# Four moved steps and a staging slot in a two-layer streaming encoder (RG-LRU layer, then forgetting attention)

## The chip, the cores and the metric

One core of a Trainium2 chip runs one program. The metric is the device time of one execution in microseconds (us). Engines are named as in the profile: PE (TensorE matmul), PEld (its weight loads), DVE (VectorE), ACT (ScalarE), POOL (GpSimd), SP (SyncE, which issues every DMA of this kernel). Each engine works through one queue, in order.

## What is computed

Two layers over a prompt of 2048 tokens and a sample group of 32 tokens, D = 1024. Each layer has modulation vectors made from a conditioning vector, a norm ahead and a norm behind:

```python
for i in range(2):
    sh, sc, gt = split3(silu(c) @ ada_w[i] + ada_b[i])       # modulation: 6 blocks n of 512 columns
    h = rmsnorm(x, norm_pre[i]) * (1 + sc) + sh
    if i == 0:  # RG-LRU: h @ w_in, conv4, gates, scan, silu gate, @ lru_w_out
        y = rglru(h)
    else:       # forgetting attention, 16 heads of 64
        q, k, v, g, fl = split(h @ fox_w_in)
        s = q @ k.T * scale + cum_q - cum_k                   # causal
        y = (softmax(s) @ v * silu(g)) @ fox_w_out            # sample group: 512 cached rows as well
    x = x + gt * rmsnorm(y, norm_post[i])
```

The sequence, the final state of the recurrence, k, v and log f are outputs.

## The kernel before

Every float32 operand of a large product is split into a high and a low part (`hi_*` on POOL, ACT or DVE, `lo_dve` on DVE, line 104), and a product is three matmuls.

The program is written as Python generators that yield after each piece of work, and a driver takes steps from them in turn. That fixes the order in which instructions are written down. The framework then lays out each engine's queue from its own planned times: whatever it expects to be ready may go ahead of what was written earlier, and what was written earlier wins when both are ready. Semaphore waits and buffer slots (named groups of equal buffers: `half` 5, `ahalf` 11, `raw` 3, `w` 5, `h` 32, `od` 5) are laid out by it too. The queues are then fixed, and an engine that reaches an instruction whose input is late stands still.

The stages in order of time:

- 0 to 100 us: constants and four modulation blocks of layer 0 (`ada`).
- about 60 to 740 us: `lru_in`, 12 column groups n for each half of the prompt, in chunks (2 a group in the first half, 3 in the second) of 48 matmuls. Beside the chunks `side` takes steps of other generators: `mod`, the other six modulation blocks (`ada`, two of layer 0, four of layer 1), and `cache_parts`. In the second half `mod` gives two steps a chunk for 16 steps and then one. A block is eight steps, one for each k; `finish` closes it: ACT copies a part out of PSUM (line 262), DVE adds twice (263, 264), and then either PE transposes the block (273) for `shv` and `gsv`, or a DMA and a product follow (n of 4 and 5). All these blocks accumulate in the one bank `pvb`.
- 740 to 1080 us: `out_tiles` of layer 0 (line 765), with the norm of layer 1.
- 1074 to 2673 us: the projections of layer 1, `proj` for each half: four groups of a v unit (line 1020) and six k, q, g units (1059). A v unit writes each of its token tiles to two staging buffers (lines 1028 and 1029, ACT) that two DMAs read (1036, 1037). The first 16 steps run before the second set of buffers is opened. Weights of the second half come in pairs, one buffer `w` and one `raw` a unit (line 952).
- 1160 to 2838 us: `attention`, merged with the projections: 8 pairs of heads p, two heads e, two query units of 512 for each half; a tile is 128 keys (lines 1239 to 1297). At the end of a unit `fin_steps` lists steps with a number of tiles to wait: `s0` copies out, `d0` and `d1` move the row of denominators through DRAM to 128 partitions (lines 1323, 1326), `rc` takes the reciprocal on DVE (1330), `d2` and `d3` send it back (1333, 1336), `zz` and `zy` multiply on POOL (1347, 1351). `sample_steps` is the same chain for the sample group (lines 1452, 1456, 1459, 1462, 1466). Whenever the next pair's projections are not done, attention starts again with loads, `LOAD_STEPS` steps of the projections, and then its maxima (1205, 1208).
- 2600 to 2716 us: `load_wout` brings the eight rows of the last matrix (line 689), splits each on ACT or POOL into `h` buffers (95, 98) and DVE (104). `out_tiles` follows (loads of line 736, split on ACT), its first seven tiles beside the attention, the rest up to the end.

Of the kernel before, what the change touches and what calls it, by code (L numbers as in the profile page):

```python
# [10 lines left out]
F32R = mybir.dt.float32r  # L11
# [24 lines left out]

V_STEPS = 16

LOAD_STEPS = 18

N_H, N_W, N_RAW, N_HALF, N_AH = 32, 5, 3, 5, 11
N_C, N_WG = 12, 2
# [12 lines left out]
def hybrid_kernel(ctx, tc, io):  # L55
# [15 lines left out]
    def get(role, shape, dt=F32):  # L71

        pool_, tag, bufs = roles[role]
        return pool_.tile(shape, dt, name=nm(tag), tag=tag, bufs=bufs)

    def set_roles(pool_, tag, bufs, *names):
        for n in names:
            roles[n] = (pool_, tag, bufs)

    def hs(shape, dt=F32):  # L80
        return get("half", shape, dt)
# [151 lines left out]
    def ada(layer, ns, acc, bank, ahead=3, whole=lambda i: False):  # L233
# [26 lines left out]
        def finish(n, ps, mod):  # L260
            lo = get("ab", [2, 512])
            act.activation(lo, ps[32:34, :], AF.Copy)
            dve.tensor_tensor(mod, mod, ps[0:2, :], ALU.add)
            dve.tensor_tensor(mod, mod, lo, ALU.add)
            if n >= 4:
                c = slice(512 * (n - 4), 512 * (n - 4) + 512)
                sp.dma_start(lo, io["npost"][layer:layer + 1, c].partition_broadcast(2))
                dve.tensor_tensor(mod, mod, lo, ALU.mult)
                sp.dma_start(gp_d[layer, :, c], mod)
                return  # L270
            pt = bank()
            for j in range(4):
                pe.transpose(pt[:, 2 * j:2 * j + 2], mod[:, 128 * j:128 * j + 128], ident[0:2, 0:2])
            ks = slice(4 * (n % 2), 4 * (n % 2) + 4)
            pt = pt[:, 0:8].rearrange("p (k g) -> p k g", g=2)
            if n < 2:
                dve.tensor_copy(shv[layer][:, ks, :], pt)
            else:
                for g in range(2):
                    dve.scalar_tensor_tensor(gsv[layer][:, ks, g], pt[:, :, g], 1.0, npre[:, layer, ks],  # L280
                                             ALU.add, ALU.mult)
# [11 lines left out]
        for i, (n, k) in enumerate(todo):  # L293
            split(i + 1)
            load(i + ahead)
            if k == 0:
                ps = acc()
            ws = parts.pop(i)
            for j, w in enumerate(ws):
                pe.matmul(ps[0:34, :], (scf if len(ws) == 1 else scs)[:, k, :], w,  # L300
                          start=k + j == 0, stop=k == KD - 1 and j == len(ws) - 1)
            if k == 3 and n not in mods:
                bias(n)
            if k == KD - 1:
                finish(n, ps, mods.pop(n))
                del ps
            yield 2 * 216

    def load_gp(layer, sample):
# [199 lines left out]
    def run(gen):  # L509
        while True:  # L510
            try:
                next(gen)
            except StopIteration as e:
                return e.value
# [167 lines left out]
    def load_wout(src, kn, w, ahead=0):  # L682
# [2 lines left out]

        def load(k):
            if k < kn:
                raw[k] = get("raw", [128, D])
                sp.dma_start(raw[k], src[128 * k:128 * k + 128, :])

        for k in range(ahead):
# [27 lines left out]
    def out_tiles(tiles, kn, zsrc, xsrc, dst, gps, bank, w, release=True, pause=0.0, post=None):  # L719
# [25 lines left out]
                zq[i][j] = (a, b)  # L745

        load(0)
        yield 2 * pause
        yield 2 * pause
        split(0)  # L750
        yield 0.0
        end = None
# [171 lines left out]
    def proj(half, h, bank):  # L924
# [66 lines left out]
        fl = None  # L991
        for i, (kind, p) in enumerate(run_units):
            ws = wsp.pop(i)
            if i == len(run_units) - 1:
                flags.add(("last", half))
                yield 0.0

# [5 lines left out]
            if kind == "v":  # L1003
# [7 lines left out]
                for t in range(nt):  # L1011
# [3 lines left out]
                    for k in range(KD):  # L1015
# [7 lines left out]
                            yield 6 * 108  # L1023
                        if c == 12:
                            drain()
                    vt, v2 = hs([128, 4, 64]), hs([128, 4, 2, 64], F32R)
                    pv = ps[:m, :256].rearrange("p (h d) -> p h d", d=64)
                    act.activation(v2[:m, :, 1, :], pv, AF.Copy)
                    act.activation(vt[:m], pv, AF.Copy)
# [78 lines left out]
    def attention(kbs, qms, vss, smp, bst, bmx, bpva, bpvb):  # L1108
# [192 lines left out]
        def fin_steps(u):  # L1301
# [34 lines left out]
                sp.dma_start(pairs[key][1][r0:r0 + 64, :], dd[1:2, :].partition_broadcast(64))  # L1336

            g = GAP[j.half]
            steps = [(0, s0), (1, d0), (1 + g, d1), (1 + 2 * g, rc), (2 + 2 * g, d2), (2 + 3 * g, d3)]
            if e == 1:  # L1340
                def ldg():
                    u.sg = get("od", [128, nq])
# [6 lines left out]
                def zy():  # L1349
# [2 lines left out]
                    sp.dma_start(z2_d[j.p, :, u.q0:u.q0 + nq], O)  # L1352
                    if u is j.last:
                        flags.add(("z", j.half, j.p))
                steps += [(2 + 2 * g, ldg), (2 + 4 * g, zz), (3 + 4 * g, zy)]
            return steps


# [2 lines left out]
        def sample_steps(p, e):  # L1361
# [106 lines left out]
            def zz():  # L1468
# [3 lines left out]
                sp.dma_start(z2_d[p, :, SEQ:TOK], O)  # L1472

            steps = [(0, load_k), (0, load_q), (1, load_v), (4, maxima), (5, fin), (7, fin2), (9, scores), (11, low),
                     (12, products), (13, s0), (14, d0), (17, d1), (20, rc), (21, d2), (24, d3)]
            return steps + ([(27 if p == NP - 1 else 32, ldg), (27 if p == NP - 1 else 36, zz)] if e else [])


# [166 lines left out]
    with tc.tile_pool(name="first", bufs=1) as first:  # L1645
# [2 lines left out]
        set_roles(big, "half", N_HALF, "ab")  # L1648
        set_roles(big, "ahalf", N_AH, "z", "zs", "xn", "hf")
        set_roles(big, "h", N_H, "aw")  # L1650
        set_roles(big, "ahalf", N_AH, "cx")
        setup()
        lc = setup_lru(first)
# [54 lines left out]
        rest[:] = run(blocks)  # L1708
        run(load_h(h, ha_d, 1, 512, 512 + NS))
        blocks, parts = later, cache_parts()  # L1710
        run(side(until(blocks, ("free", 0, 1, 0)), [[(islice(mod, 16), 2), (mod, 1)], [(parts, 2)]]))
        for _ in range(4):
            next(wout)
        rest = run(blocks)
# [7 lines left out]
        last = ada(1, (4, 5), bpvb, bank0, ADA_LAST, lambda i: True)  # L1722
        for _ in range(4):
            next(wout)
        next(out)
        next(out)
        for fn in rest:
# [38 lines left out]
    set_roles(second, "od", N_OD, "od")  # L1766
    set_roles(big, "raw", N_RAW, "z")
    set_roles(big, "w", N_W, "zs", "gp")
    set_roles(big, "half", N_HALF, "hf")
    att = {}  # L1770
    last_banks = cycle(bst, bst, bpj, bpj)

# [3 lines left out]
    def main():  # L1776
# [12 lines left out]
            yield next(b)  # L1789
        yield from until(b, ("last", 1))  # L1790
        w = [{}, {}]
        wout = load_wout(io["w3"], NP, w, 2)
        yield next(wout)
        yield from b
        yield from wout
# [104 lines left out]
```

## Time and profile before

| | |
|---|---|
| median of 3 runs | 3016.19 us (3014.15 to 3018.24) |
| profiled execution | 3012.26 us, span 3010.5 us |
| PE busy | 2860.8 us, 95% of the span |
| DVE, ACT, POOL busy | 61%, 49%, 42% |
| DMA | 548 MB, 182 GB/s in the mean |

A row of the windows view gives a stretch's length, each engine's busy time (with the number of its instructions), the granted TensorE clock as a share of 2.4 GHz, the DMA engines' busy share and the rate. A row of the timeline gives start, duration, engine (SPq is SP's queue, a DMA issue), line, operation, out<-in, shape and count; in brackets the engine's idle time before it and what ended it.

### The profile page before, as it was taken

Reading aid. Unit: us, or ns where it says so; the run is one execution under the profiler, and the core shown is the slowest. Engines: PE = TensorE matmul, PEld = TensorE weight load, DVE = VectorE, ACT = ScalarE, POOL = GpSimd, SP = SyncE. Lnnn points to the kernel's source line nnn. Section 1 sums busy time; section 2 is a strip of 40 time slices with the busy share of each in tenths; the row PEclk is TensorE's granted clock in tenths of the full one; section 3 lists DMA queues with packets and bytes.
Section 4 is the critical chain, followed back from the end, with each engine's and each line's share of the span. In section 5 each row is a group of like instructions: output and inputs, shape, how many; then the busy total and the mean of one; then the engine's idle time right before and its main releaser. Section 6 shows DMA issues by size and latency. Waiting matters only on the chain. (4 is left out here: it accounts for less than half of the span.)

```text
span 3010.5 us, 45166 instructions
## 1 busy us (share of the span) xinstructions
PE 2860.8 (95%) x14948; PEld 2290.1 (76%) x14948; DVE 1843.2 (61%) x3282; ACT 1488.2 (49%) x2996; POOL 1257.2 (42%) x1156
## 2 busy tenths in 40 slices
PE   6999999999999989999999999999999999989998
PEld 3777888888676777777777778887888888856686
DVE  7678767777633335646464575676666766677422
ACT  6565544455444423534353443565665656556411
POOL 5444434333322222434343332554555545556522
PEclk8999999999999999999999999999999999999999
DMA  7655586444644598676767865676556655555343
GB/s 262 225 202 203 180 280 212 155 152 138 194 150 139 173 316 253 196 236 193 233 189 228 252 195 176 142 193 162 140 159 152 172 157 154 130 138 123 89 147 97
DMA packets 407002, 548.40 MB, mean 182 GB/s; under 512 B 77096, under 2 KB 241064, under 8 KB 406768
## 3 DMA queue, kind: packets, MB, share of 16 engines
q1 hardware_dynamic: 406768, 545.50, 60.4%
q8 instruction: 119, 1.95, 0.3%
q14 instruction: 115, 0.94, 0.1%
HBM read 333.13 MB, written 212.22 MB: 181 GB/s over the span
## 5 line engine op out<-in xcount | busy, mean ns | idle before, releaser
L1268 POOL TENSOR_TENSOR ahalf<-ahalf,ahalf 128x512 f32<-128x512 f32 (+2 forms) x528 | 586.4, 1111 | 411.6 <-ACT ahalf L1245 400.4
L1059 PE MATMUL pj<-h,w 128*128 128x512 f32 (+1 forms) x2304 | 593.6, 364 | 0.0
L1245 ACT ACTIVATE ahalf<-st 128x512 fp32r<-128x512 f32 (+3 forms) x640 | 341.7, 534 | 386.8 <-PE st L1243 324.1
L104 DVE TENSOR_TENSOR ahalf<-st,ahalf 128x512 fp32r<-128x512 f32 (+3 forms) x640 | 386.6, 605 | 206.1 <-ACT st L1246 179.5
L1059 PEld LDWEIGHTS pj<-h,w 128*128 128x128 f32 x2304 | 423.6, 190 | 85.4 <-issue 0.6
L1208 DVE TENSOR_REDUCE mxs<-mx 128x1 f32<-128x512 f32 (+3 forms) x640 | 371.4, 604 | 132.4 <-PE mx L1205 87.0
L1246 ACT ACTIVATE st<-st 128x512 f32<-128x512 f32 (+3 forms) x640 | 339.5, 530 | 0.0
L1239 PE MATMUL st<-ahalf,kv 128*128 128x512 f32 (+3 forms) x640 | 246.3, 385 | 32.0 <-DVE ahalf L104 30.7
L1291 PE MATMUL pva<-ahalf,vs 128*128 128x512 f32 (+3 forms) x640 | 241.8, 389 | 11.0 <-ACT ahalf L1245 7.3
L1243 PE MATMUL st<-ahalf,kb 96*128 96x512 f32 (+3 forms) x640 | 243.4, 386 | 4.1 <-ACT ahalf L1226 3.7
L1020 PE MATMUL pj<-w,h 128*128 128x256 f32 (+3 forms) x1296 | 229.6, 289 | 11.2 <-DVE flog L1035 6.5
L1205 PE MATMUL mx<-kb,qm 96*128 96x512 f32 (+3 forms) x640 | 224.8, 382 | 7.8 <-DMA qm<-q_d 3.3
L1292 PE MATMUL pvb<-ahalf,vs 128*65 128x512 f32 (+3 forms) x640 | 228.4, 366 | 3.2 <-DVE od L1320 2.1
L573 PE MATMUL pj<-h,w 128*128 128x512 f32 (+1 forms) x1032 | 224.5, 366 | 0.6 <-DVE h L104 0.3
L1020 PEld LDWEIGHTS pj<-w,h 128*128 128x128 f32 (+1 forms) x1296 | 191.5, 189 | 22.5 <-issue 8.6
L573 PEld LDWEIGHTS pj<-h,w 128*128 128x128 f32 x1032 | 174.7, 189 | 32.6 <-DVE h L104 1.3
L573 PE MATMUL st<-h,wg 128*128 128x512 f32 (+1 forms) x840 | 187.6, 377 | 2.3 <-DVE wg L104 1.5
L1059 PE MATMUL pj<-h,raw 128*128 128x272 f32 (+1 forms) x576 | 188.5, 327 | 0.0
L104 DVE TENSOR_TENSOR w<-raw,w 128x1024 fp32r<-128x1024 f32 (+2 forms) x61 | 86.6, 1420 | 153.5 <-ACT w L95 92.0
L104 DVE TENSOR_TENSOR ahalf<-ahalf,ahalf 128x512 fp32r<-128x512 f32 (+2 forms) x183 | 143.4, 785 | 57.9 <-POOL ahalf L98 25.5
L1239 PEld LDWEIGHTS st<-ahalf,kv 128*128 128x128 f32 x640 | 121.6, 190 | 74.4 <-DVE ahalf L104 53.8
L573 PEld LDWEIGHTS st<-h,wg 128*128 128x128 f32 x840 | 147.8, 192 | 32.1 <-DVE wg L104 2.7
(330 smaller groups left out, 5566.2 us busy)
## 6 DMA issues: line engine op xcount, KB each, us to landing
wp_d<-w SPq DMA_DIRECT2D x60, 512.0 KB
vs<-v_d SPq DMA_DIRECT2D x96, 256.0 KB
kv<-k_d SPq DMA_DIRECT2D x192, 128.0 KB
ahalf<-q_d SPq DMA_DIRECT2D x192, 128.0 KB
raw<-in_w SPq DMA_DIRECT2D x44, 512.0 KB
hb_d<-wg SPq DMA_DIRECT2D x32, 512.0 KB
v_d<-half SPq DMA_DIRECT2D x64, 256.0 KB
raw<-wp_d SPq DMA_DIRECT2D x30, 512.0 KB
```

What stands on the lines that cost most here:

```text
L104: dve.tensor_tensor(o, i, f(h), ALU.subtract)
L573: pe.matmul(ps[:, :b - a], l, cols(r, a, b), start=i == 0, stop=i == 23)
L1020: pe.matmul(ps[:m, :nw], l, r, start=c == 0, stop=c == 23)
L1059: pe.matmul(ps[:, :b - a], l, cols(r, a, b), start=c == 0, stop=c == 23)
L1208: dve.tensor_reduce(u.mxs[:sw, si, c:c + 1], ps[:sw, :kw], axis=AX.X, op=ALU.max)
L1239: pe.matmul(ps[:kw, c0:nq], j.ka[k0 // 512][:, kc:kc + kw], u.qa[:, c0:nq], start=True, stop=False)
L1243: pe.matmul(ps[:kw, c0:nq], j.kb[k0 // HALF][0:96, kd:kd + kw], u.qb[0:96, c0:nq], start=False, stop=True)
L1245: act.activation(ph[:kw, c0:nq], ps[:kw, c0:nq], AF.Exp, scale=0.125)
L1246: act.activation(ps[:kw, c0:nq], ps[:kw, c0:nq], AF.Exp, scale=0.125)
L1268: pool.tensor_tensor(u.acc[:kw, c0:nq], f(ph)[:kw, c0:nq], u.acc[:kw, c0:nq], ALU.add)
L1291: pe.matmul(u.pva[:, c:nq], vs[:kw, 0:128], ph[:kw, c:nq], start=ti == 0, stop=last)
L1292: pe.matmul(u.pvb[0:65, c0:nq], vs[:kw, 64:129], pl[:kw, c0:nq], start=ti == 0, stop=False)
```

## The change

Seven edits. (1) `ada`: `finish` ends after its additions, and a new `finish2` does the rest one step later; a block is nine steps, and `mod` now gives two steps a chunk for 26 steps. (2) The v unit's staging buffers have a role of their own, `vst`: slots `ahalf` in the first 16 steps, `half` as before after them. (3) `rc` and all that follows it stand three tiles later in the list, in the second half and for the sample group (not for its last pair). (4) `LOAD_STEPS` 18 to 24. (5) `load_wout` for the last matrix asks for three rows ahead, even rows in `w` slots, and starts one unit earlier. (6) `out_tiles` has a third pause between its first load and its first split; layer 0 takes the third step at once. (7) The flag "last" is set a unit earlier, which is what starts (5).

```diff
-LOAD_STEPS = 18
+LOAD_STEPS = 24
@@ ada: finish
             dve.tensor_tensor(mod, mod, lo, ALU.add)
+            return lo
+
+        def finish2(n, mod, lo):
             if n >= 4:
...
             if k == KD - 1:
-                finish(n, ps, mods.pop(n))
+                mod = mods.pop(n)
+                lo = finish(n, ps, mod)
                 del ps
+                yield 0.0
+                finish2(n, mod, lo)
+                del mod, lo
             yield 2 * 216
@@ load_wout: load
-                raw[k] = get("raw", [128, D])
+                raw[k] = get("w" if ahead and k % 2 == 0 else "raw", [128, D])
@@ out_tiles
         load(0)
-        yield 2 * pause
-        yield 2 * pause
+        for _ in range(3):
+            yield 2 * pause
         split(0)
@@ proj
-            if i == len(run_units) - 1:
+            if i == len(run_units) - 2:
                 flags.add(("last", half))
...
-                    vt, v2 = hs([128, 4, 64]), hs([128, 4, 2, 64], F32R)
+                    vt, v2 = get("vst", [128, 4, 64]), get("vst", [128, 4, 2, 64], F32R)
@@ attention: fin_steps
-            steps = [(0, s0), (1, d0), (1 + g, d1), (1 + 2 * g, rc), (2 + 2 * g, d2), (2 + 3 * g, d3)]
+            a = 1 + 2 * g + (3 if j.half else 0)
+            steps = [(0, s0), (1, d0), (1 + g, d1), (a, rc), (a + 1, d2), (a + 1 + g, d3)]
...
-                steps += [(2 + 2 * g, ldg), (2 + 4 * g, zz), (3 + 4 * g, zy)]
+                steps += [(a + 1, ldg), (a + 1 + 2 * g, zz), (a + 2 + 2 * g, zy)]
@@ attention: sample_steps
-                     (12, products), (13, s0), (14, d0), (17, d1), (20, rc), (21, d2), (24, d3)]
+                     (12, products), (13, s0), (14, d0), (17, d1)]
+            steps += [(20, rc), (21, d2), (24, d3)] if p == NP - 1 else [(23, rc), (24, d2), (27, d3)]
             return steps + ([(27 if p == NP - 1 else 32, ldg), (27 if p == NP - 1 else 36, zz)] if e else [])
@@ driver
+        set_roles(big, "ahalf", N_AH, "vst")
...
-        run(side(until(blocks, ("free", 0, 1, 0)), [[(islice(mod, 16), 2), (mod, 1)], [(parts, 2)]]))
+        run(side(until(blocks, ("free", 0, 1, 0)), [[(islice(mod, 26), 2), (mod, 1)], [(parts, 2)]]))
...
+        next(out)
...
-    set_roles(big, "half", N_HALF, "hf")
+    set_roles(big, "half", N_HALF, "hf", "vst")
...
-        wout = load_wout(io["w3"], NP, w, 2)
+        wout = load_wout(io["w3"], NP, w, 3)
```

## Rows read from the trace of the kernel before

**Rows 1.** The page's first part: engines, busy time, share of the span.
```profile
PE 2860.8 (95%) x14948; PEld 2290.1 (76%) x14948; DVE 1843.2 (61%) x3282; ACT 1488.2 (49%) x2996; POOL 1257.2 (42%) x1156
```

**Rows 2.** Windows around six stops of PE; columns as in the profile section.
```profile
472.00:490.00 18.00, 14.21 (x92) 13.85 (x91) 10.21 (x16) 3.99 (x9) 5.12 (x4) 0.81 0.54 170
560.00:574.00 14.00, 10.71 (x70) 10.18 (x69) 7.90 (x10) 3.23 (x7) 3.57 (x2) 0.88 0.38 125
1088.00:1110.00 22.00, 15.46 (x106) 15.08 (x105) 3.83 (x12) 3.35 (x9) 7.14 (x21) 0.84 1.01 336
1805.00:1816.00 11.00, 7.73 (x53) 7.27 (x51) 2.85 (x6) 0.80 (x2) 0.00 (x0) 0.84 0.51 156
2638.00:2656.00 18.00, 12.17 (x43) 9.19 (x42) 9.43 (x15) 6.46 (x12) 6.67 (x6) 0.81 0.64 173
2704.00:2722.00 18.00, 12.46 (x44) 8.85 (x44) 10.71 (x21) 7.65 (x14) 9.18 (x10) 0.81 0.60 124
```

**Rows 3.** Timeline, 476 to 567 us: the ends of two modulation blocks.
```profile
479.72 0.58 PE L273 MATMUL pj<-ident,half 2*128 2x2 f32 x4 [3.79 <-DVE half L264]
...
562.81 3.15 DVE L626 TENSOR_TENSOR c<-c,c 128x1024 f32<-128x1024 f32 x1
...
566.79 0.63 PE L300 MATMUL pvb<-ahalf,scs 128*34 128x512 f32 x2 [3.29 <-DVE half L263]
```

**Rows 4.** Windows, second half of the LRU layer: two modulation steps a chunk, then one.
```profile
380.00:460.00 80.00, 76.42 (x421) 64.32 (x420) 55.29 (x66) 36.13 (x49) 30.90 (x26) 1.00 0.80 280
460.00:720.00 260.00, 251.07 (x1518) 226.18 (x1517) 186.31 (x268) 133.81 (x199) 92.17 (x69) 0.98 0.48 159
```

**Rows 5.** Timeline, 1099 to 1103 us: first v unit.
```profile
1099.49 0.39 ACT L1029 ACTIVATE half<-st 128x256 f32<-128x256 f32 x1 [6.18 <-DMA out_v_o<-half]
...
1102.76 1.47 PE L1020 MATMUL pj<-w,h 128*128 128x272 f32 x5 [5.34 <-DVE flog L1035]
```

**Rows 6.** Timeline, 2638 to 2712 us: the last matrix and the first tile's load.
```profile
2638.89 0.46 SPq L689 DMA_DIRECT2D raw<-in_w  x1
...
2644.00 0.62 POOL L98 TENSOR_SCALAR h<-raw 128x512 fp32r<-128x512 f32 x1 [6.06 <-DMA raw<-in_w]
...
2701.72 0.42 SPq L736 DMA_DIRECT2D raw<-z_d  x1
...
2711.58 1.06 ACT L95 ACTIVATE w<-raw 128x1024 fp32r<-128x1024 f32 x1 [5.40 <-DMA raw<-z_d]
```

**Rows 7.** Line 952 by operation: durations in ns, first and last start.
```profile
L952 SPq DMA_DIRECT2D w<-wp_d x32: 319/469/637, 1660.6 to 2522.1; - x32
L952 SPq DMA_DIRECT2D raw<-wp_d x32: 319/416/1397, 1662.5 to 2574.0; - x32
```

**Rows 8.** Timeline, 2434 to 2503 us: reciprocal chains of two units.
```profile
2434.92 0.34 SPq L1466 DMA_DIRECT2D tiny<-sg_d  x1
...
2436.27 0.30 SPq L1459 DMA_DIRECT2D dns_d<-rc  x1
...
2436.67 0.37 SPq L1326 DMA_DIRECT2D rc<-dn_d  x1
...
2442.38 0.18 DVE L1330 RECIPROCAL rc<-rc 128x4 f32<-128x4 f32 x1 [3.72 <-DMA rc<-dn_d]
...
2500.82 0.34 SPq L1326 DMA_DIRECT2D rc<-dn_d  x1
...
2502.76 0.30 SPq L1459 DMA_DIRECT2D dns_d<-rc  x1
```

**Rows 9.** Windows around seven waits of line 1330: one of them, and their sum.
```profile
2438.00:2452.00 14.00, 11.82 (x69) 10.40 (x69) 6.88 (x14) 6.66 (x14) 6.88 (x8) 0.88 0.60 124
...
sum 74.00, PE 63.48 PEld 53.45 DVE 32.78 ACT 35.95 POOL 37.27; mean PE 9.07 PEld 7.64 DVE 4.68 ACT 5.14 POOL 5.32
```

**Rows 10.** Timeline, 1810 us: the first maximum of the second half.
```profile
1810.30 0.76 PE L1205 MATMUL mx<-kb,qm 96*128 96x512 f32 x1 [3.27 <-DMA qm<-q_d]
```

**Rows 11.** Waits of POOL, 1838 to 2840 us: total, times, longest.
```profile
POOL od L1347 <- DMA od<-dn_d: 2.5, 2, 1.3
```

## Prediction

> **What bounds the kernel now.** I read the page first: PE is busy for 95% of the span, the next engine for 61% [rows 1]. The sum of PE's work is not touched by any edit, so only PE's standing time is at stake, and the time it spends at half clock after a stop. Next I listed every idle stretch of PE over 0.6 us with what ended it, and looked at the largest in the windows view. The reader is to take two numbers from a window: its length less PE's busy time, and one less the granted clock, times the length. The second is what the lower of the two clock levels (1.2 instead of 2.4 GHz) cost there, for at half speed half of the time is lost: a clock of 0.81 over 18 us is 6.8 us at half, 3.4 us lost. Each stop is then followed back in the timeline to the instruction that came late.
>
> **1. Modulation blocks in two steps.** At 479.72 PE stood 3.79 us before the transposes of line 273, because DVE's additions came late; at 566.79 it stood 3.29 us before the next block's first matmul, which needs the bank `pvb` that the late addition still reads [rows 3]. DVE was late because a product that it works on beside POOL took 3.15 us [rows 3]. With the clock the two cost 3.79 + 3.42 and 3.29 + 1.68: 12.2 us [rows 2]. In the new order a step, in this stretch a chunk of 5.5 to 10 us of matmuls (48 of 272 or 512 columns), stands between the additions and the transposes, and one more before `pvb` is wanted; both exceed the lateness. PE is always supplied there (251.07 us of 260 [rows 4]), so the planner has no idle moment into which it would pull the transposes forward. I count 85%: 10.4 us. The first four blocks run with nothing between the steps, so nothing changes there. What `finish2` takes along (the DMAs and the product for n of 4 and 5, DVE's copies for the rest) is wanted after 740 us at the earliest; the cover is the rest of the LRU layer.
> The price is the pace: six blocks take 54 steps instead of 48, and 13 chunks instead of 8 take two. The eight chunks at two steps left PE idle for 3.58 us, 0.45 each; the slower stretch after it for 8.93, of which 7.08 are the two stops, leaving 0.07 for each of some 25 chunks [rows 4]. Five chunks more at 0.38: 1.9 us.
>
> **2. Staging slots.** Two buffers a tile out of five `half` slots hold two tiles. At 1099.49 ACT had stood 6.18 us until a DMA out of such a buffer had landed, and PE 5.34 us for the bank behind it [rows 5]; the window's loss is 6.54 + 3.52 = 10.1 us [rows 2]. Four tiles now go to `ahalf`, whose other users there (layer 0's last tiles) are done by then. But DMA is full in this stretch (share 1.01 [rows 2]), so the landings stay late, and tiles 5 to 8 have the five slots again. I take 7; bounds 3 (one of the two stops) and 10.1.
>
> **3. Last matrix, and the pause before the first split.** A row's load issued at 2638.89 was waited for by POOL until 2644.00 [rows 6]; DVE and then PE stood behind that, 5.83 + 3.42 = 9.3 us [rows 2]. The load was late because `raw` has three slots and the last projection weights took them up to then; these loads run out at 2522.1 for `w` and only at 2574.0 for `raw` [rows 7]. Even rows in `w` are thus loaded long before their buffers in `h` come free, and odd rows get a `raw` slot one row sooner. The number of rows ahead alone would matter little, as SP issues what has a slot. 85%: 7.9 us.
> The next stop is the tile load of 2701.72, for which ACT stood 5.40 us until 2711.58 [rows 6]; PE lost 5.54 + 3.42 = 9.0 us [rows 2]. Its `raw` slot comes free earlier now, but the load took 9.9 us and ACT came to it after 4.5: where the load moves, the planner's place for ACT moves too, unless the `w` slots that the split writes to, now shared with four rows, hold it back. One third: 3.0 us. The third pause only moves the split in the written order.
>
> **4. `LOAD_STEPS`.** One restart shows a stop: 3.27 us for `qm` [rows 10], with the clock 5.0 [rows 2]. That maximum had been pulled ahead of written projections, so six more steps may or may not move it. One third: 1.7. Elsewhere the longer pause is filled by projections.
>
> **5. Reciprocals three tiles later.** Seven units in the second half show DVE standing at line 1330 (3.72 us in the one shown [rows 8]) and PE behind it. The seven windows have 74 less 63.48 = 10.5 us of idle PE, and three of them a dip of 1.68 us [rows 9]: 15.6 us. Is it won? The lists give tiles, but the queues do not keep them: the load of line 1466 stands at place 32 of its list and was issued at 2434.92, ahead of line 1459, which stands at 21 [rows 8]. What is ready goes first, and rc becomes ready by the planner's reckoning soon after `d1`, in the old list and in the new. What the seven have in common is another thing: line 1326 was issued 0.4 us after line 1459's write, and its data let DVE go only 5.7 us later; where it went first (2500.82 before 2502.76) DVE did not wait [rows 8]. The edit moves both alike. I take 0, bounds 0 and 15.6.
> The Trainium skill (DMA: Bandwidth & Descriptors, Queues, rings and completion order) says that a DMA's semaphore increment lands only after every earlier write of that DMA engine; the trace agrees, 5.7 us behind the write and no wait where the read went first [rows 8]. By that rule too the stop goes only if the two change places.
>
> **The sum.** 10.4 + 7 + 7.9 + 3.0 + 1.7 = 30.0. Less 1.9 for the pace, and 2 for new small stops, an estimate from the 2 us that PE idled in the slower stretch of [rows 4]: 26. The profiled execution took 3012.26 us (span 3010.5); 2986 against it. The median of the runs lies 3.9 us above that execution: 2990.
>
> **Rivals.**
> (a) Reciprocals do come late enough: all 15.6 us as well, 2974. For it: seven stops of one kind, 3.72 us in the one shown, and three tiles are more: the two issues of line 1326 shown are 28 tiles and 64.2 us apart, 2.3 us a tile, 6.9 for three [rows 8]. Against it: [rows 8]. The skill's page on DMA (Rules for kernel authors) says to issue early and to wait late, which would give this time; the trace does not show that the place in the list is where the wait falls. 13%.
> (b) The waits are dealt again. Every queue after 380 us is planned anew; loads that land later than planned stop an engine elsewhere. Then of 3 to 5 nothing stays, of 1 and 2 10.4 + 7, and half of those 17.4 us is given back in new stops of the kind of [rows 10]: some 8 us won, 3008. For it: DMA times of 5 to 10 us against places planned after 4.5. Against it: slots and a chunk of matmuls are real room, whatever the order. 19%.
> (c) Slower: the products `zz` on POOL. They follow `d3`, which follows rc. Now POOL waits for them twice, 2.5 us in all, in 1000 us [rows 11]. If rc, `d2` and `d3` do move by three tiles (6.9 us) while `zz` keeps its place in POOL's queue, POOL stands, and a stop of POOL of that length cost PE 9.3 us at 2641 [rows 2, 6]. There are 16 such products in the second half. From three of them on the gain is gone, from four the kernel is slower; five would give 2990 + 46 = 3036. Against it: the queues follow readiness, `zz` with them. 9%.
> (d) Something not named, on either side: 4%.
>
> **How the numbers follow.** The forecast, 2990, has 55%, and its own range is 2976 to 3004 (all bounds of 2 at once with a half of the uncertain thirds). About 0.2% can be told from no change here, 6 us: faster is below 3010. Faster: 55 + 13 + about 10 of (b) + 1 = 79%; the same: 9 of (b) and 1 = 10%; slower: 9 + 2 = 11%. The range reaches down past (a), 2968 with all bounds won, and up past (b), 3014; it leaves out (c) and the ends of the others.
>
> **What will show it.** Right: no idle over 1 us at lines 273 and 300 after 460 us, full clock there; ACT's line 1029 without 5 us waits near 1090, and the window of the first v unit at 1.00; POOL's line 98 on `h<-raw` without a wait for a DMA; line 1330 still waiting 2 to 4 us in some units of the second half, those where line 1326 follows line 1459. Wrong: if line 1330 waits nowhere the lists do set the place, and (a) holds; if PE stops behind POOL's line 1347, (c); if the six windows are clean and the time is above 3005, the loss has gone to stops that the rows don't name.

## The result, and the profile after

The changed kernel took 2988.47 us (median of 4 runs, 2986.51 to 2997.05) beside 3016.31 us for the kernel before (4 runs, 3014.15 to 3018.24): a ratio of 0.9913, 95% interval 0.9893 to 0.9934. That is 28 us won by the medians, 26 by the ratio. On another chip, where the kernel before took 3010.86 us, it took 2980.94 us, ratio 0.9902 (0.9889 to 0.9915). The forecast was 2990.0 us. The total was met; three of the five terms of the sum behind it were not, and most of what follows is about them. Edits in the texts set off below are numbered as in the section on the change; the points of the last table and after it are numbered as in the prediction.

The profiled execution took 2988.29 us, span 2986.6 us. The page's first part, to be held against [rows 1]:

```profile
PE 2851.6 (95%) x14948; PEld 2289.9 (77%) x14948; DVE 1827.7 (61%) x3282; ACT 1483.5 (50%) x2995; POOL 1255.2 (42%) x1156
```

The same work on every engine, and PE still busy for 95%. Windows of the kernel after around its largest stops (columns as in the profile section ahead), and the stretch of [rows 4]:

```profile
490.00:508.00 18.00, 14.91 (x85) 13.57 (x84) 11.34 (x18) 6.31 (x10) 7.81 (x7) 0.91 0.32 112
526.00:542.00 16.00, 12.55 (x77) 11.93 (x76) 9.96 (x13) 6.72 (x12) 5.77 (x3) 0.89 0.24 88
1088.00:1116.00 28.00, 21.95 (x113) 19.32 (x112) 9.84 (x27) 5.25 (x12) 8.87 (x22) 0.82 0.89 307
1798.00:1811.00 13.00, 8.06 (x42) 7.50 (x42) 2.98 (x6) 0.80 (x2) 0.00 (x0) 0.74 0.50 157
2620.00:2660.00 40.00, 35.83 (x187) 27.76 (x185) 36.69 (x61) 25.52 (x52) 25.43 (x24) 1.00 0.75 182
2700.00:2720.00 20.00, 16.88 (x74) 12.36 (x73) 13.32 (x28) 11.13 (x25) 13.13 (x12) 0.91 0.48 127
...
460.00:720.00 260.00, 252.02 (x1526) 226.14 (x1525) 181.68 (x265) 133.60 (x199) 87.23 (x69) 0.99 0.47 154
```

Read against [rows 2]: the last matrix's stretch, 2620 to 2660, is at full clock with small stops. The other places still have a stop each: two in the LRU layer (at 497 and 530 us instead of 476 and 563), one in the first v unit (6.05 us idle, clock 0.82), one at the restart near 1800 us (4.94 us idle, clock 0.74; it was 3.27 us and 0.84 in [rows 2, 10]), and one of 2.99 us at 2706 us.

Where the 23.9 us between the two spans went, with PE's idle time and what the lower clock level cost, worked out for each stretch as in the prediction from the stops and the granted clock of both traces (up to PE's last matmul):

| stretch (us of before) | idle + clock before | after | won |
|---|---|---|---|
| 0 to 742, up to the end of the LRU layer | 49.1 + 17.1 | 49.0 + 15.4 | 1.8 |
| 742 to 1177, layer 0's tiles, v unit, first attention unit | 11.8 + 5.1 | 11.3 + 5.1 | 0.5 |
| 1177 to 2624, attention beside projections | 52.4 + 13.6 | 49.0 + 15.3 | 1.7 |
| 2624 to the end | 28.3 + 13.6 | 17.6 + 6.8 | 17.5 |

The rows add up to 21.5 of the 23.9 us; the rest the reckoning does not place. So in this pair of traces about three quarters of the gain lie behind 2624 us, where the forecast had put 10.9 of 26. The place is not the same in every trace: cut at the end of the last projection instead (2672.7 us before), 7.8 us are won in the attention beside the projections and 11.3 behind them in this trace, but 18.8 and 10.4 in the trace of the second measurement, whose span is 2976.5 us.

### The profile page after: what moved, and what is told of

It reads as the page before. It is cut to its first block, busy times and chain, and to the rows that moved or that the text cites. A ratio compares the mean times of both kernels' runs of the same rounds, so it can differ in the third digit from the quotient of the medians.

```text
span 2986.6 us, 45134 instructions
## 1 busy us (share of the span) xinstructions
PE 2851.6 (95%) x14948; PEld 2289.9 (77%) x14948; DVE 1827.7 (61%) x3282; ACT 1483.5 (50%) x2995; POOL 1255.2 (42%) x1156
## 3 DMA queue, kind: packets, MB, share of 16 engines
q8 instruction: 119, 1.95, 0.3%
## 5 line engine op out<-in xcount | busy, mean ns | idle before, releaser
L1275 POOL TENSOR_TENSOR ahalf<-ahalf,ahalf 128x512 f32<-128x512 f32 (+2 forms) x528 | 579.9, 1098 | 386.5 <-ACT ahalf L1252 362.8
L1066 PE MATMUL pj<-h,w 128*128 128x512 f32 (+1 forms) x2304 | 594.5, 365 | 4.8 <-DVE flog L1042 4.7
L1066 PEld LDWEIGHTS pj<-h,w 128*128 128x128 f32 x2304 | 426.4, 191 | 93.6 <-issue 5.4
L1246 PE MATMUL st<-ahalf,kv 128*128 128x512 f32 (+3 forms) x640 | 244.9, 383 | 21.9 <-DVE ahalf L104 20.3
L580 PE MATMUL pj<-h,w 128*128 128x512 f32 (+1 forms) x1080 | 233.9, 366 | 0.6 <-DVE h L104 0.3
L580 PEld LDWEIGHTS pj<-h,w 128*128 128x128 f32 x1080 | 182.7, 190 | 34.0 <-DVE h L104 1.3
L580 PEld LDWEIGHTS st<-h,wg 128*128 128x128 f32 x864 | 149.7, 188 | 31.8 <-DVE wg L104 2.8
L104 DVE TENSOR_TENSOR ahalf<-ahalf,ahalf 128x512 fp32r<-128x512 f32 (+2 forms) x183 | 134.3, 735 | 60.3 <-ACT ahalf L95 27.8
```

The source lines that it names most:

```text
L104: dve.tensor_tensor(o, i, f(h), ALU.subtract)
L580: pe.matmul(ps[:, :b - a], l, cols(r, a, b), start=i == 0, stop=i == 23)
L1066: pe.matmul(ps[:, :b - a], l, cols(r, a, b), start=c == 0, stop=c == 23)
L1246: pe.matmul(ps[:kw, c0:nq], j.ka[k0 // 512][:, kc:kc + kw], u.qa[:, c0:nq], start=True, stop=False)
L1275: pool.tensor_tensor(u.acc[:kw, c0:nq], f(ph)[:kw, c0:nq], u.acc[:kw, c0:nq], ALU.add)
```

## The experiments

All ratios are to the kernel before in runs beside; the changed kernel stands for reference at 0.9902 as above. No kernel leaves out any part of the computation.

### The edits one by one

**Modulation alone.**

```
+            return lo
+        def finish2(n, mod, lo):
...
-        ... islice(mod, 16), 2 ...
+        ... islice(mod, 26), 2 ...
```

> The kernel before with edit (1) alone (finish in two steps, two modulation steps a chunk for 26 steps). By the forecast's sum: 10.4 us won, 1.9 lost to the pace, so 8.5 us faster than the kernel before. By what the trace of the changed kernel shows up to the end of the LRU layer (2 to 3 us ahead there; stops of 3.1 and 3.5 us in front of the gate products at 497 and 530 us in place of the two removed): 1 to 4 us faster, which is no difference by the 0.2% bound. The trace tells them apart: in the first case no stop over 2 us between 460 and 600 us, in the second the stops have another line and the same size.

Measured: 0.9985 (0.9973 to 0.9997), 4.5 us faster (0.9 to 8.1). The window of [rows 4] in this kernel:

```profile
460.00:720.00 260.00, 254.33 (x1545) 227.70 (x1544) 183.69 (x274) 137.25 (x203) 92.02 (x71) 0.99 0.45 154
```

Idle 5.67 us and some 2.6 us for the clock, against 8.93 and 5.2 in [rows 4]: about 5.9 us won in the layer, between the two expectations. The stops have the other line that the second expectation named, 2.63 and 2.17 us, at two thirds of the size of the two that went. What they are is seen in the timeline of the kernel after, 496 to 501 us:

```profile
496.85 1.09 ACT L620 ACTIVATE c<-c 128x1060 f32<-128x1060 f32 x1 [6.87 <-DVE c L626]
497.95 1.28 ACT L667 ACT_TABLE_LOAD   x1
...
499.74 0.55 ACT L596 ACTIVATE c<-pva,prm 128x354 f32<-128x354 f32 x1
...
500.34 0.43 PE L595 MATMUL pva<-c,half 128*128 128x354 f32 x1 [3.09 <-ACT c L596]
```

ACT waited 6.87 us for DVE, then worked through line 620, a table load and line 667 before it could empty the bank (line 596) that PE's gate product (595) needs. The late engine is not that of [rows 3]. DVE had no long product here: it stood itself, 4.49 us for POOL's line 98 and 2.51 us for POOL's line 617, and POOL had stood 5.35 us for a DMA out of a `w` buffer (`cache_parts`):

```profile
492.03 0.41 POOL L98 TENSOR_SCALAR w<-ahalf 128x256 fp32r<-128x256 f32 x1 [5.35 <-DMA v_d<-w]
...
493.56 1.95 POOL L617 TENSOR_TENSOR c<-c 128x1060 f32<-128x1060 f32 x1
...
495.55 1.26 DVE L619 SCALAR_TENSOR_TENSOR c<-c,c 128x1060 f32<-128x1060 f32 x1 [2.51 <-POOL c L617]
```

Ahead of the stop at 530 us it is the same chain, with 4.14 us for that DMA. So the two stops of [rows 3] are gone, and another chain, with POOL at its head, stops PE in the same stretch.

**The pace, in the changed kernel.**

```
-        ... islice(mod, 26), 2 ...
+        ... islice(mod, 16), 2 ...
```

> The changed kernel with two modulation steps a chunk for 16 steps again instead of 26. By the forecast the pace costs 1.9 us: 2 us faster than the changed kernel, and the blocks, still in two steps, show no stop. If the two stops of 2.9 and 3.0 us in front of the gate products at 495 and 528 us belong to the pace (two steps a chunk there, where the kernel before had one): both go, with a dip each, up to 8 us faster. If they belong to DVE and ACT whatever the pace is, they stay: 0.

Measured: 0.9933 (0.9919 to 0.9947), where two other variants of the changed kernel beside it (below) had 0.9905 and 0.9909: some 8 us slower, which none of its theories expected. Its windows first, then those of the changed kernel in its second measurement (2976.5 us):

```profile
460.00:720.00 260.00, 253.00 (x1544) 227.08 (x1543) 190.84 (x268) 135.69 (x199) 95.01 (x71) 1.00 0.45 152
730.00:820.00 90.00, 83.03 (x327) 52.30 (x326) 55.74 (x85) 45.50 (x81) 26.90 (x20) 0.98 0.62 196
```

```profile
460.00:720.00 260.00, 252.64 (x1524) 226.96 (x1523) 179.77 (x269) 136.46 (x201) 86.52 (x69) 0.98 0.46 152
730.00:820.00 90.00, 87.02 (x363) 56.94 (x362) 64.16 (x83) 44.60 (x81) 36.38 (x26) 1.00 0.66 197
```

With the old pace the stop at 530 us is gone and that at 497 us is 1.56 us. Yet PE's idle time in the whole stretch is the same, 7.00 us against 7.36, for smaller stops take their place. Full clock against 0.98 looks like 5 us more for the faster pace; but the changed kernel without the third pause, which differs nowhere in this layer, has 7.04 us of idle at full clock there. The traces show no more than the forecast's 1.9 us for the pace: with the old one the layer ends at 734.3 us, in the seven traces with the new one between 733.1 and 739.1, 736.8 in the mean. But nine steps a block at the old pace do not end within the layer. The rest runs after it, with nothing beside, and 730 to 820 us loses 6.97 + 1.8 = 8.8 us instead of 2.98. There PE meets the old stop again, at the last block's transposes:

```profile
744.10 0.41 PE L276 MATMUL st<-ident,half 2*128 2x2 f32 x4 [1.93 <-DVE half L264]
```

From the end of the layer to the first v unit this kernel takes 338.1 us, the seven others 329.6 to 331.8: some 7 us, which is most of the 8 us by the runs. The rest is within what two traces differ by.

**Staging slots alone.**

```
-                    vt, v2 = hs([128, 4, 64]), hs([128, 4, 2, 64], F32R)
+                    vt, v2 = get("vst", [128, 4, 64]), get("vst", [128, 4, 2, 64], F32R)
```

> The kernel before with edit (2) alone (the v unit's staging buffers from the ahalf slots in the first 16 steps). By the forecast: 7 us faster (bounds 3 and 10). By the trace of the changed kernel, in which PE stands 1.25 and 4.65 us at 1094 and 1107 us behind the same flog addition: the stop is moved by a few tiles, 0 (within 2 us of the kernel before), and ACT again waits some 5 to 6 us for a DMA out of a half buffer, after the first unit's eighth tile.

Measured: 1.0006 (0.9995 to 1.0017), no difference. The timeline, in the same place as [rows 5]:

```profile
1104.21 0.38 ACT L1029 ACTIVATE half<-pj 128x256 f32<-128x256 f32 x1 [6.12 <-DMA out_v_o<-half]
...
1105.90 2.47 PE L1059 MATMUL pj<-h,w 128*128 128x512 f32 x5 [5.26 <-DVE flog L1035]
```

The wait of [rows 5], 6.18 us for the DMA out of a `half` buffer, is there with 6.12 us, some tiles later, at the end of the unit: PE now stands before the K unit (line 1059).

**All eight tiles in `ahalf`**, in the changed kernel.

```
-    set_roles(big, "half", N_HALF, "hf", "vst")
+    set_roles(big, "half", N_HALF, "hf")
@@ proj, end of the first v unit
+                    if half == 0:
+                        set_roles(big, "half", N_HALF, "vst")
```

> The changed kernel with the first v unit's staging buffers in ahalf slots for all eight tiles instead of the first four (then half as before). If the stop before the K unit (4.65 us and a dip at half clock after it) is there because tiles 5 to 8 have the five half slots again, it goes: 4.65 us, the 1.25 us one ahead of it and some 5 us of half clock, 8 to 10 us faster than the changed kernel. If the landing of the DMAs in a stretch where all DMA engines are busy sets it, the stop stays, 0 to 2 us.

Measured: 0.9908 (0.9891 to 0.9925), the same as the changed kernel beside it. The windows of this kernel, then of the changed kernel (second measurement):

```profile
1088.00:1116.00 28.00, 25.17 (x142) 21.16 (x141) 15.63 (x46) 6.30 (x14) 9.00 (x22) 1.00 0.78 262
1234.00:1250.00 16.00, 13.24 (x60) 10.68 (x59) 11.60 (x21) 4.80 (x12) 9.94 (x10) 0.79 0.83 253
```

```profile
1088.00:1116.00 28.00, 21.94 (x103) 18.75 (x103) 12.28 (x39) 5.42 (x12) 8.88 (x22) 0.82 0.85 284
1234.00:1250.00 16.00, 13.55 (x80) 10.99 (x80) 12.82 (x24) 6.74 (x16) 10.26 (x10) 1.00 0.77 265
```

The first theory is right about the stop of 4.65 us: with slots for all tiles it is gone (the one of 1.25 us ahead of it stays, 1.26 us), 3.2 us of idle and 5.0 of clock in that window. The total does not move. In the trace 3.4 us come back as a dip at 1241 us, and others behind 2600 us; whether the earlier start brings these about or they are scatter, one trace of each kernel can't say.

**Last matrix, flag and pause alone.**

```
+                raw[k] = get("w" if ahead and k % 2 == 0 else "raw", [128, D])
+            if i == len(run_units) - 2:
+        for _ in range(3):
+        wout = load_wout(io["w3"], NP, w, 3)
```

> The kernel before with edits (5) to (7) alone (three rows ahead, even rows in w slots, the flag a unit earlier, the third pause). By the forecast: 7.9 + 3.0 = 10.9 us faster, of which the second half is the least certain. By the trace of the changed kernel, which gained some 19 us between 2618 and 2840 us: 17 to 21 us faster, with both windows (2641 and 2708 in the kernel before) clean and the dip at 2687 gone. If it is well below 17, the gain there needs the other edits too, through the reciprocal's place at the end of the attention.

Measured: 0.9963 (0.9948 to 0.9977), 11.1 us faster (6.9 to 15.7): the forecast's size, not the 19 us of the trace after. Its windows, for the last two of [rows 2] and the stretch between:

```profile
2638.00:2656.00 18.00, 15.79 (x83) 12.54 (x82) 15.55 (x24) 11.45 (x23) 11.06 (x10) 1.00 0.95 242
...
2660.00:2690.00 30.00, 26.78 (x117) 19.72 (x116) 22.99 (x48) 15.03 (x35) 13.92 (x13) 0.79 0.41 117
...
2704.00:2722.00 18.00, 14.45 (x61) 10.59 (x60) 11.89 (x22) 10.38 (x20) 12.77 (x12) 0.89 0.59 156
```

The first window lost 9.3 us and loses 2.2; the third lost 9.0 and loses 5.5. Between them is what is left: 3.2 us of idle and 6.3 of clock, around the first split of a tile, which still waits for its load. In the kernel before the same stretch lost 2.7 and 1.2:

```profile
2660.00:2690.00 30.00, 27.33 (x147) 20.67 (x148) 27.01 (x53) 18.93 (x42) 17.03 (x16) 0.96 0.49 152
```

```profile
2663.65 0.37 SPq L736 DMA_DIRECT2D raw<-z_d  x1
...
2669.18 1.06 ACT L95 ACTIVATE w<-raw 128x1024 fp32r<-128x1024 f32 x1 [3.17 <-DMA raw<-z_d]
...
2670.29 0.80 PE L765 MATMUL pj<-h,w 128*128 128x512 f32 x1 [1.45 <-ACT w L95]
```

**Without the third pause**, in the changed kernel.

```
-        for _ in range(3):
-            yield 2 * pause
+        yield 2 * pause
+        yield 2 * pause
```

> The changed kernel without the third pause (edit 6). By the forecast the pause moves a split in the written order only: within 1 us of the changed kernel. If it is what keeps the first split of the second layer's tiles behind its load, ACT waits longer than 1.0 to 2.0 us for that load there and PE behind it: 3 to 9 us slower.

Measured: 0.9905 (0.9890 to 0.9920), beside 0.9909 for the variant with `LOAD_STEPS` at 30 and 0.9902 for the changed kernel on another chip: no difference that these runs can tell. ACT waits 1.23 us for that load. Within that the pause is worth nothing, as forecast.

**Reciprocals alone.**

```
+            a = 1 + 2 * g + (3 if j.half else 0)
+            steps = [(0, s0), (1, d0), (1 + g, d1), (a, rc), (a + 1, d2), (a + 1 + g, d3)]
```

> The kernel before with edit (3) alone (reciprocals three tiles later in the list). By the forecast: 0, and line 1330 (a few lines on in this kernel) still stands 2 to 4 us in some seven units of the second half. By its rival (a): 15.6 us faster and no such wait. By the trace of the changed kernel, where five such waits of 1.5 to 3.0 us are left in the second half instead of seven: 2 to 6 us faster.

Measured: 1.0015 (1.0002 to 1.0028): slower, by 0.6 to 8.4 us. Its 12 runs had a mean granted clock of 0.9816, the 31 of the kernel before beside them 0.9835; over 3010 us that is 5.7 us at most, the size of the difference. In its trace PE stands less than in the kernel before (140.8 us in all against 149.7) and loses more to the clock (57.1 against 52.2).

**The changed kernel again, and without the reciprocals' edit.**

> The changed kernel itself, beside the kernels that leave one edit out. The four edits measured alone give -0.15, +0.06, -0.37 and +0.15%: with nothing from LOAD_STEPS they add up to 0.9969, 9 us. Theory A (the edits add up, and a part of the first measurement's 28 us was that chip's and those runs' own): 0.995 to 0.998 here. Theory B (the edits help each other at the end of the attention, or LOAD_STEPS gives the rest): 0.990 to 0.993, as first measured.

> The changed kernel without edit (3): the reciprocals back at their old tiles. By the forecast (queues go by what is ready): within 2 us of the changed kernel. If edit (3) helps edit (5) at the end of the attention, where the changed kernel gained 8 us more between 2656 and 2690 us than edits (5) to (7) did alone: 8 us slower than the changed kernel. By rival (a): 15 us slower.

Measured: 0.9902 (0.9889 to 0.9915) and 0.9908 (0.9896 to 0.9921). Theory B for the first: the gain is as large as first measured. For the second 1.8 us slower, give or take 5.5: the runs show no worth of the edit in the changed kernel. Rival (a) of the prediction has fallen with both runs.

### `LOAD_STEPS`

```
-LOAD_STEPS = 18
+LOAD_STEPS = 24
```

The changed kernel with 18, the kernel before with 24, and the changed kernel with 30:

> The changed kernel with LOAD_STEPS at 18. By the forecast 1.7 us slower than the changed kernel. By the changed kernel's trace, where the stop for qm at the restart is 4.94 us instead of 3.27: 0 to 2 us faster than the changed kernel. If LOAD_STEPS is what the single edits lack: 10 us or more slower.

> The kernel before with edit (4) alone (LOAD_STEPS 24). By the forecast: 1.7 us faster. In the changed kernel the same edit is worth 11 us (taking it away gave 0.9939 against 0.9902), of which 7 fell between 2644 and 2670 us, where the first tile load of the second layer is issued. Theory A: it is worth that by itself, since the projections end earlier in any order: 9 to 12 us faster. Theory B: it needs edits (5) to (7), because without them the last matrix's rows still come late at 2641 and the tiles cannot start earlier: 0 to 4 us faster, with the stops of POOL's line 98 and ACT's line 95 as in the kernel before.

> The changed kernel with LOAD_STEPS 30. If every six steps bring the projections' end some 5 to 10 us forward and all of that is won: another 8 to 11 us faster than the changed kernel. If the gain was that the first tile's load had landed when ACT came to it, which is nearly so with 24 (ACT waits 1.0 us instead of 3.2): within 3 us of the changed kernel, with no wait of ACT's line 95 for that load.

Measured: 0.9939 (0.9926 to 0.9952) without it, 11 us slower than the changed kernel (5.6 to 16.7); 0.9966 (0.9954 to 0.9978) with it alone, 10.2 us faster (6.6 to 13.8) than the kernel before; 0.9909 (0.9894 to 0.9925) with 30, no further gain. Theory A of the second: the edit is worth that by itself. Of the two signs named with theory B, ACT's wait for the first tile's load is still there (4.44 us, and PE stands 4.29 us behind it), while POOL's line 98 no longer waits for a row. With 30 the second theory held: ACT waits 0.24 us for that load, and nothing more is won. There the last projection ends at 2627.8 us instead of 2643.1 (changed kernel, second measurement), but the stretch behind it takes 352.2 us instead of 333.5. The largest single edit beside the last matrix was the one that the forecast had at 1.7 us.

A part of where it acts is seen in the list of PE's waits (total, times, longest). The wait of the score products for DVE's low parts, in the kernel before, with 24 alone, in the changed kernel with 18, and in the changed kernel (second measurement):

```profile
PE st L1239 <- DVE ahalf L104: 30.7, 36, 5.8
```

```profile
PE st L1239 <- DVE ahalf L104: 20.2, 33, 2.1
```

```profile
PE st L1246 <- DVE ahalf L104: 27.5, 34, 2.4
```

```profile
PE st L1246 <- DVE ahalf L104: 18.1, 29, 2.2
```

10.5 and 9.4 us less. It is not scatter: the total is 27.4 to 30.7 us in the six traces with 18 and 15.6 to 20.3 in the seven with 24. Nor is it the gain as it stands. PE's idle time in all fell by 6.3 us (149.7 to 143.4) with 24 alone and by 11.6 (141.9 to 130.3) in the changed kernel, for other waits grow: that of line 1225 for DVE from 5.2 to 10.2 us in the first case. With 30 the wait above is 22.7 us again, at the same time of the kernel. And in the kernel before the 5.8 us are one stop, the one at the last matrix of [rows 2, 6]:

```profile
2647.51 0.79 PE L1239 MATMUL st<-ahalf,kv 128*128 128x512 f32 x1 [5.83 <-DVE ahalf L104]
```

With 24 alone no stop of PE between 2595 and 2700 us exceeds 1.86 us. Some 5 to 7 us of the fall are small stops between 1100 and 1800 us, the longest of 2.1 us (10.3 us in all before, 4.9 with 24 alone; 11.8 and 5.0 in the changed kernel with 18 and 24). One of them in the kernel before: the next score product has to wait until ACT and DVE have passed on a tile, and PE has three projection products (line 1059) to fill that time.

```profile
1423.13 0.60 ACT L1245 ACTIVATE ahalf<-st 128x512 fp32r<-128x512 f32 x1
1423.33 0.86 PE L1059 MATMUL pj<-h,w 128*128 128x512 f32 x3
1423.62 0.59 ACT L1246 ACTIVATE st<-st 128x512 f32<-128x512 f32 x1
1424.32 0.68 DVE L104 TENSOR_TENSOR ahalf<-st,ahalf 128x512 fp32r<-128x512 f32 x1
...
1425.05 0.44 PE L1239 MATMUL st<-ahalf,kv 128*128 128x384 f32 x1 [0.86 <-DVE ahalf L104]
```

That the longer pause deals the projections out so that more such places are filled is argued from the sums; it was not traced stop by stop, and how the 10 us are made up stays open.

A smaller part may be the reciprocals. DVE's waits at that line, 1800 to 2660 us: the kernel before; reciprocals' edit alone; 24 alone; the changed kernel with 18; without the reciprocals' edit; the changed kernel.

```profile
DVE rc L1330 <- DMA rc<-dn_d: 24.8, 9, 3.8
```

```profile
DVE rc L1330 <- DMA rc<-dn_d: 22.4, 8, 3.7
```

```profile
DVE rc L1330 <- DMA rc<-dn_d: 14.3, 8, 3.3
```

```profile
DVE rc L1337 <- DMA rc<-dn_d: 22.6, 8, 3.9
```

```profile
DVE rc L1337 <- DMA rc<-dn_d: 15.5, 9, 3.3
```

```profile
DVE rc L1337 <- DMA rc<-dn_d: 14.2, 8, 3.0
```

These waits of DVE shrink by 7 to 11 us wherever `LOAD_STEPS` is 24, and stay wherever it is 18, with the reciprocals' edit or without. What PE has of it is less: its waits for DVE's low parts between 1815 and 2600 us, behind the restart and ahead of the last matrix, go from 10.3 to 7.7 us with 24 alone and from 9.6 to 7.8 in the changed kernel. The reason for the shorter waits is in SP's order. Of the 25 or 26 reads of the denominators (line 1326) in that stretch, 7 were issued within 3 us behind a sample write (1459) in each of the six traces with 18, and 4 in each of the eight with 24 or 30. DVE waited over 1 us behind 71 of these 74 reads, and behind 11 of the 285 others. In the kernel before such a read landed 5.1 to 5.7 us after its issue, the others after 1.6 to 4.4. The six steps shift the sample chain against the units by enough to part some of the pairs.

## Why the forecast held, point by point

The total came out 1.5 us from the forecast, because errors of both signs cancelled. That it came so near is luck: the mechanism held for point 5 and the first part of 3, and failed for 1, 2 and 4.

| edit | forecast, us won | alone | taken from, or in, the changed kernel |
|---|---|---|---|
| 1 modulation, with its pace | 8.5 | 4.5 (0.9 to 8.1) | old pace: 8 slower, as blocks run late |
| 2 staging slots | 7 | -1.8 (-5.1 to 1.5) | not taken out |
| 3 last matrix, flag, pause | 10.9 | 11.1 (6.9 to 15.7) | pause: no difference |
| 4 `LOAD_STEPS` | 1.7 | 10.2 (6.6 to 13.8) | 11 (5.6 to 16.7) |
| 5 reciprocals | 0 | -4.5 (-8.4 to -0.6) | 1.8 (-3.7 to 7.3) |
| small stops | -2 | | |
| sum | 26 | 19.5, give or take 8.4 | all together: 29.5 (25.6 to 33.4); first measurement 26 (20 to 32) |

(Shares of 3010 us; the uncertainty of the sum is the root of the squared half intervals.)

**1.** The stops at lines 273 and 300 went, as forecast: what is left of them after 430 us is 1.58 us, at 442 us. The step that failed is "I count 85%", the reading that a stop with room put behind it is a stop won. Between 430 and 742 us PE stands 9.5 to 10.8 us in the five traces with the old `finish` and 9.7 to 11.5 in the seven of the changed kernel and its variants at the new pace: as much as before, now in front of the gate products and in smaller stops (with edit (1) alone it is 7.7). What fell there is the loss to the clock, from 5.1 to 6.8 us to between 0 and 5.1. The full clock that the prediction named as a sign is not there in most of these traces (0.91 and 0.89 around the two new stops in the kernel after). The price of the pace, 1.9 us, is not contradicted by the traces. The reason given for the lateness holds for one of the two stops: ahead of the first, at 476.56 us, the product named took 1.21 us, and what was long was a low part of 2.63 us. The net gain is half of what was counted.

**2.** The step that failed is "I take 7". The sentence before it, that the landings stay late and tiles 5 to 8 have the five slots again, was the right one, and its consequence is not the lower bound of 3 but zero: the stop was moved by slots for four tiles, and went with slots for all eight. The window's clock of 1.00 that the prediction named as a sign came only then. And even then the total did not move: the bound to put below was nothing.

**3.** Held in size, 10.9 against 11.1, and in its first part, 7.1 us won in its window for 7.9. The wait of POOL's line 98 is small: in the kernel after it waits once for a row's load, 0.61 us in the first trace and 2.3 in the second, instead of 6.06. Of the first tile's load the forecast gave one third; with edits (5) to (7) alone ACT still waits 3.17 us for it and the stretch around it costs 9.5 us instead of 3.9, more than the 3.5 won at 2704 us: of that third nothing is won by these edits alone. So the near match of the total is in part chance, for the three windows together account for 5.0 us of the 11.1. That the pause is worth nothing was right.

**4.** This term was mis-sized the most, 1.7 us against 10.2 measured alone. The failed step is the choice of what to look at. The list of stops was cut at 0.6 us, and a change of pace at every restart was priced by the one restart that showed a stop, 3.27 us for `qm` [rows 10]. That stop stayed, and was 4.94 us after. "Elsewhere the longer pause is filled by projections" put all other places at nothing without a sum behind it: the pause shifts all of the projections' work against the scores, and in some thirty waits, most of them under 2.5 us, PE stood about 10 us less, of which other waits took a part back. With this edit alone the row's wait of [rows 6], counted in point 3, goes too. In the changed kernel it also brought the first tile's load forward. With 18, and after with 24:

```profile
2658.81 0.37 SPq L743 DMA_DIRECT2D raw<-z_d  x1
...
2664.35 1.06 ACT L95 ACTIVATE w<-raw 128x1024 fp32r<-128x1024 f32 x1 [3.18 <-DMA raw<-z_d]
...
2665.46 0.80 PE L772 MATMUL pj<-h,w 128*128 128x512 f32 x1 [1.45 <-ACT w L95]
```

```profile
2656.57 0.38 SPq L743 DMA_DIRECT2D raw<-z_d  x1
...
2659.72 0.43 SPq L743 DMA_DIRECT2D raw<-z_d  x1
...
2661.51 1.06 ACT L95 ACTIVATE w<-raw 128x1024 fp32r<-128x1024 f32 x1 [0.98 <-DMA raw<-z_d]
...
2663.64 1.08 PE L772 MATMUL pj<-h,w 128*128 128x512 f32 x4
```

The last projection ends at 2653.6 us against 2658.8, the loads of two tiles follow each other at once, and PE has other work until the split is done. That is the uncertain third of point 3, won by points 3 and 4 together: with either alone ACT still waits for that load, 3.17 and 4.44 us.

**5.** Held: the list's place does not set the queue's, and line 1330 goes on waiting where its read follows a sample write. The Trainium skill's rule (DMA: Bandwidth & Descriptors, Queues, rings and completion order), an increment lands after every earlier write of that DMA engine, fits the traces: in the 14 of this case, 71 of the 82 waits over 1 us stand behind such a write. What the forecast missed is that another edit parts the pairs. That the edit alone is a little slower (0.6 to 8.4 us) goes with a lower granted clock in its runs; what lowers it was not found.

**Rivals.** (a) fell. (b), the waits dealt again, is what happened to points 1 and 2, and the other way round to 4: there the new deal was the gain. (c) fell: POOL's waits for the same DMA are 4.6 us in three, not 2.5 in two [rows 11], and PE has no wait for that line of POOL's.

**Open.** The edits alone add up to 19.5 us, give or take 8.4, and together they give 29.5 (give or take 3.9) by the second measurement and 26 (give or take 6) by the first. Against the second the 10 us between lie just outside what the intervals allow, against the first the difference lies inside. So it is not shown that the edits help each other. One place where they would is seen, the first tile's load, which needs points 3 and 4 together; the rest was not traced.

## What to carry to other kernels

A step that changes the phase of two streams of work cannot be priced by the stops that are visible at its place: sum the waits of the whole stretch by line and releaser, small ones too, and ask which of them depend on what runs side by side. More buffers for a loop that waits for a transfer can move the wait to the first iteration that is short again; count the iterations before a gain is written down. Where a change gives room to one late chain, look for the next chain that can stop the same engine, and compare the idle time of the whole stretch, not the stop that went.

## What the runs showed of the hardware

Two executions of the changed kernel with the same instructions had spans of 2986.6 and 2976.5 us, at a mean granted clock of 0.985 and 0.988. At the lower level half of the time is lost, so that is 0.015 times 2986.6 = 44.8 us against 35.7, 9 us apart. Not all of that is the difference: PE's busy time differs by 5.4 us (2851.6 and 2846.2) and its idle time by the other 4.7. About half of the spread between these two traces is slower matmuls.

A dip is no simple price of a stop. In the changed kernel with `LOAD_STEPS` 18 a stop of 1.45 us at 2664 us and one of 1.05 us at 2673.5 us are each followed by time at the lower level, and the shorter one by more; in the changed kernel's second measurement 30 us with more standing time, 4.57 us with one stop of 1.95 us, stay at the higher one:

```profile
2660.00:2674.00 14.00, 11.45 (x49) 7.50 (x47) 10.36 (x23) 7.15 (x17) 7.02 (x6) 0.88 0.33 98
2674.00:2690.00 16.00, 15.08 (x59) 11.74 (x60) 11.19 (x21) 9.97 (x22) 7.38 (x7) 0.68 0.45 106
```

```profile
2640.00:2670.00 30.00, 25.43 (x124) 17.37 (x125) 28.28 (x55) 18.60 (x41) 15.74 (x14) 1.00 0.50 136
```

By the clocks of the first two windows the stop of 1.45 us was followed by a loss of 1.7 us and that of 1.05 us by one of 5.1; the one of 1.95 us by none. A dip read beside a stop in one trace, as the forecast took it for each of its windows, is not a fixed part of that stop's price.
